# Modulation vectors on VectorE, attention scores on two row halves, and another order in the first mixer of a three-block forward pass

## The chip, the core and the metric

One NeuronCore of a Trainium2 chip runs the whole program: TensorE (PE; PEld is its weight load), VectorE (DVE), ScalarE (ACT), GpSimd (POOL) and SyncE (SP), which issues most DMAs. The metric is the device time of one execution in microseconds, as the median of several runs. TensorE's clock has two levels, 1.2 and 2.4 GHz; the profile gives the granted clock of a stretch as a fraction of the higher one. Everything is float32. Each product is made of three fp32r matmuls on a high and a low part of each operand (hi·hi, hi·lo, lo·hi), added up in PSUM.

## What is computed

A first block of three sub-blocks (feed-forward, mixer, feed-forward) acts on 512 rows of 1024 features; then come two layers, each with a mixer and a feed-forward. 256 context rows go beside the first of them. Each sub-block's input is normalized and changed by modulation vectors, which are products of one conditioning vector with large matrices. The part that the change touches:

```
# first mixer: 8 heads of 64, a band of 9 chunks of 64 keys, and a gated recurrence
q, k, v, xr, yr, g_att, g_rec = split(h @ w_in)
att = chunked_attention(q, k, v, rel_bias) @ w_att_o      # softmax(q k^T / 8 + bias) v
rec = (rg_lru(conv(xr), ...) * gelu(yr)) @ w_rec_o
merged = sigmoid(g_att) * att + sigmoid(g_rec) * rec

# layer mixers: 512 own keys and 256 context keys, head dimension 64
s = einsum('bqhgd,bkhd->bhgqk', gq, gk) * ATTN_SCALE      # 8 query heads, 2 key heads
p = softmax(s); o_g = einsum('bhgqk,bkhd->bqhgd', p, gv)
s = einsum('bqhjd,bkhjd->bhjqk', dq, dk) * ATTN_SCALE     # 4 heads of two score maps
a = softmax(s)[:, :, 0] - lam * softmax(s)[:, :, 1]; o_d = einsum('bhqk,bkhe->bqhe', a, dv)

# 27 modulation vectors of 1024, each silu(c) @ w[:, c0:c0+1024] + b
mod = (silu(c) @ w_ada + b_ada), (silu(c) @ w_mod + b_mod)
```

## The kernel before

The stages follow each other: a start (0 to 38 us of the profiled span), the first feed-forward (to 411), the first mixer (to 899), the second feed-forward with the context's mixer woven in (to 1585), the mixer of layer 0 (to 2310), its feed-forward (to 2913), the mixer of layer 1 (to 3638) and its feed-forward.

**Weights.** A step of the program (`Step`) names the weight blocks (`Unit`) that it needs. SP loads each block of 128x1024 into one of five `raw` buffers (L243 waits for a free one), in the order of the steps. `split` makes the high part on ScalarE (L282) and the low part on VectorE by a subtraction (L283). Products go through L309 to L311 and L321 to L323, and `esplit` splits a result (L326 on ScalarE, L328 or L330 on VectorE).

**Modulation vectors.** `mod` makes a vector out of eight pieces, each a plain `raw` block of 128x1024. `pieces` scales it by one column of the conditioning vector and adds it up: on GpSimd a scaling of the first (L383), and for each later one a scaling (L387) and an addition (L388); its other branch, on VectorE, is one fused multiply-add. `start` makes the first two vectors on VectorE by the same means (L405, L407). `turn` and `fin` then sum over the partitions and bring the row into shape. The vectors' steps are woven into the stages' bodies by `weave`, by each step's cost.

**Order.** Steps are merged by cost (`merge`, `weave`); within the program the order on PE, ACT and DVE is set by a scheduler at compile time, on SP and POOL it is as written. Each engine runs its instructions in order.

**First mixer** (`mixer1`). `front` runs the first products. Of `s_yr`, the eight products of the recurrent gate (Gelu at L787), four were its items; the other four, the values (`s_v`) and the queries and keys of the first pair of heads followed. Then 16 attention jobs (a head, and two query tiles) run through `skew`, whose stages are scores (L852) and the softmax's exponential (L862), scaling (L866 to L868), transposes (L1027), products with the values (L1051, L1052), and a fold (L1057 to L1063). `TUNE["soft"]["m"]` sets the order of these stages. The steps of the jobs were cut in four; three parts were merged with the queries and keys of the next pair (six products), the last with four steps of the recurrent part `s_rec` (convolution at L902 to L908, split at L910).

**Layer mixers** (`attend`). A job of "gqa" was one head and two query tiles; `scores` (L1313) wrote a bank `big` with products on one 64-row half, then the second bank. The keys `R["gk"]` held key head 0 on rows 0 to 63 and key head 1 on rows 64 to 127, and the query heads were laid out to match. In "diff" a job is a head and a query tile with both score maps, one on each half, and their banks were written one after the other. There are two `big` banks and four `mm` banks in PSUM.

Of the kernel before, what the change touches and what calls it, by code (L numbers as in the profile page):

```python
# [10 lines left out]
BF16 = mybir.dt.bfloat16  # L11
# [4 lines left out]
D = 1024  # L16
# [25 lines left out]
for _name, _w in (("qn", 64), ("kn", 64), ("dl", 256)):  # L42
# [24 lines left out]
    "soft": {"m": "scptf", "gc": "sptcf", "g0": "sptcf", "g1": "spctf", "dc": "scptn", "d0": "stcnp", "d1": "snptc"},  # L67
# [92 lines left out]
class K:  # L160
# [30 lines left out]
    def pair(self, n=512, kind=None):  # L191

        if n == 256:
            return self.half(F32R, kind).rearrange("p (a n) -> p a n", a=2)
        return self.s((2, n), F32R)

# [141 lines left out]
    def mod(self, key, w, c0, bias, ccol, gain=None, mult=None):  # L338
# [27 lines left out]
        steps = self.pieces(key, w, c0, ccol, begin, self.POOL)  # L366
# [407 lines left out]
    def mixer1(self, a, hk, yk, last):  # L774
# [7 lines left out]
        items = []  # L782
        for c, u in enumerate(self.units_a(w_in, 2560, D)):
# [4 lines left out]
            items.append((u, fn))  # L788
        items, s_yr = items[:4], [self.one(T, u, act, d) for u, d in items[4:]]
# [20 lines left out]
        s_qk = {}  # L810
        s_at = {}
        src = w_in.rearrange("(k p) c -> p k c", p=128)
        for i in range(4):
            us = [self.unit(src[:, :, j + i * 128:j + (i + 1) * 128]) for j in (0, 512)]
            s_qk[i] = []
            for j, u in enumerate(us):
                def fn(w, i=i, j=j):
                    ps = self.mm()
                    self.mma(ps, w, 0, act)
                    p = qk[i, j] = self.pair()  # L820
                    self.esplit(ps, p[:, 0, :], p[:, 1, :], 0.125 if j == 0 else 1.0)
                s_qk[i].append(Step(fn, [u]))
# [191 lines left out]
        steps += merge(cut[3], s_rec[:nr]) + drain  # L1014
# [50 lines left out]

    def skew(self, jobs, order, st_s, st_c, st_t, st_p, st_f=None, st_n1=None, st_n2=None):
# [5 lines left out]
        stages = [x for c in order for x in kinds[c]]  # L1072
        n, last = len(jobs), max(d for d, _, _ in stages)
        out = [[]]
        for i in range(n + last):
            for k, (d, f, pe) in enumerate(stages):
# [4 lines left out]
                if k == 0 and i < n:  # L1081
                    out.append([])
        steps, drain = out[:n], out[n]
        return steps, drain
# [52 lines left out]
    def rotate(self, out, x, nh, c, sn):  # L1137
# [4 lines left out]
        DVE.tensor_tensor(out, x, c.unsqueeze(1).to_broadcast([128, nh, 64]), ALU.mult)  # L1142
# [6 lines left out]
        DVE.tensor_tensor(out, out, t.rearrange("p (h d) -> p h d", h=nh), ALU.add)  # L1149
# [16 lines left out]
    def to_feat(self, src, T, scale=1.0, kind=None):  # L1166
# [4 lines left out]
        p = self.pair(T, kind)  # L1171
# [24 lines left out]
    def kv_gqa(self, w, T, act, rope, R, save=None):  # L1196
# [3 lines left out]
        def done(box):  # L1200
            gv = R["gv"] = self.pair(T).rearrange("p a n -> p (a n)").rearrange("p (t v x d) -> p t v x d", v=2, x=2, d=64)
            tk = self.e(T).rearrange("p (t d) -> p t d", d=128)
# [3 lines left out]
            for t, x in enumerate(self.head_norm([o[:, 0:128] for o in box["o"]], 2)):  # L1206
                o = tk[:, t, :].rearrange("p (h d) -> p h d", h=2)
                if rope:
                    self.rotate(o, x, 2, E["tab"][:, 1, 0, t, :], E["tab"][:, 1, 1, t, :])
# [746 lines left out]
```

## Time and profile before

| | us |
|---|---|
| median of three runs | 4000.06 |
| the three runs, from and to | 3992.86 to 4002.28 |
| the profiled execution, its own time | 4003.47 |
| its span in the trace | 4001.7 |

One execution was profiled. The views used below are the page with the busy time of each engine and the costliest groups of instructions, windows of busy time by stage (with the mean granted clock), groups by line with mean durations, single lines with minimum, median and maximum, waits, and the timeline of a stretch. In a group, `out<-in` are the program's tile names, `x` is a count, and the last column is idle time of the engine ahead of the group with what ended it.

### The profile page before, as it was taken

What the parts mean: (1) busy time and instruction counts of PE and PEld (TensorE: products, weight loads), DVE (VectorE), ACT (ScalarE), POOL (GpSimd) and SP (SyncE); (2) the same over time, 40 slices, a digit from 0 to 9 for tenths busy, and PEclk for the clock granted to TensorE, in tenths of its full rate; (3) what the DMA queues carried; (4) which work ended last, traced back from release to release, by engine and by line L of the source; (5) the groups of instructions that cost most, each with busy time, mean ns of one, the idle gap of its engine ahead of it and who ended that gap; (6) DMA issues with size and microseconds to landing.
All of it is one profiled execution on the core that took longest, in us unless ns stands there. A gap on an engine that the chain in (4) does not pass through costs nothing. (4 is left out here: it accounts for less than half of the span.)

```text
span 4001.7 us, 50668 instructions
## 1 busy us (share of the span) xinstructions
PE 3773.1 (94%) x19612; PEld 3196.3 (80%) x19612; DVE 2514.3 (63%) x3347; ACT 1533.9 (38%) x2437; POOL 1394.0 (35%) x1133
## 2 busy tenths in 40 slices
PE   7999987999899999899999989999998999899999
PEld 5888866778788887778887878888887887688887
DVE  5343478846766665957667466767587776655344
ACT  4222345533354443235433334333332543334322
POOL 1341364315844332451323144543146132312100
PEclk9999988999999999999999989999999999899999
DMA  6554533446455655221333356666532123333432
GB/s 226 155 160 128 152 113 116 145 127 194 149 160 173 187 168 176 80 82 41 106 95 95 121 166 198 195 200 195 170 104 82 56 85 96 106 121 114 127 103 94
DMA packets 534050, 536.26 MB, mean 134 GB/s; under 512 B 19696, under 2 KB 435696, under 8 KB 533808
## 3 DMA queue, kind: packets, MB, share of 16 engines
q1 hardware_dynamic: 517088, 487.48, 40.1%
q0 software_dynamic: 16720, 45.53, 3.5%
q8 instruction: 154, 2.52, 0.3%
q14 instruction: 88, 0.72, 0.1%
HBM read 507.66 MB, written 25.28 MB: 133 GB/s over the span
## 5 line engine op out<-in xcount | busy, mean ns | idle before, releaser
L283 DVE TENSOR_TENSOR wlo<-raw,whi 128x1024 fp32r<-128x1024 f32 (+3 forms) x674 | 921.9, 1370 | 803.1 <-ACT whi L282 783.6
L282 ACT ACTIVATE whi<-raw 128x1024 fp32r<-128x1024 f32 (+3 forms) x674 | 694.1, 1032 | 1551.6 <-PE mm L310 649.5
L309 PE MATMUL mm<-hT,whi 128*128 128x512 f32 (+1 forms) x2384 | 910.8, 385 | 44.4 <-ACT hT L326 11.0
L310 PE MATMUL mm<-hT,whi 128*128 128x512 f32 (+1 forms) x2384 | 907.1, 382 | 17.9 <-DVE hT L328 17.9
L311 PE MATMUL mm<-hT,wlo 128*128 128x512 f32 (+1 forms) x2384 | 902.9, 380 | 0.0
L309 PEld LDWEIGHTS mm<-hT,whi 128*128 128x128 f32 x2384 | 460.4, 195 | 132.4 <-ACT hT L326 14.0
L310 PEld LDWEIGHTS mm<-hT,whi 128*128 128x128 f32 x2384 | 463.2, 195 | 99.3 <-DVE hT L328 20.5
L311 PEld LDWEIGHTS mm<-hT,wlo 128*128 128x128 f32 x2384 | 462.6, 194 | 83.4 <-issue 0.4
L388 POOL TENSOR_TENSOR s<-s,raw 128x1024 f32<-128x1024 f32 x189 | 495.6, 2622 | 15.8
L387 POOL TENSOR_SCALAR raw<-raw,csil 128x1024 f32<-128x1024 f32 x189 | 281.4, 1489 | 380.9 <-DMA raw<-in_w_mod 191.2
L322 PE MATMUL mm<-wlo,s 128*128 128x512 f32 (+1 forms) x1004 | 371.4, 371 | 4.6 <-DVE wlo L283 4.6
L321 PE MATMUL mm<-whi,s 128*128 128x512 f32 (+1 forms) x1004 | 369.1, 371 | 0.0
L323 PE MATMUL mm<-whi,s 128*128 128x512 f32 (+1 forms) x1004 | 368.9, 370 | 0.0
L309 PE MATMUL mm<-s,whi 128*128 128x256 f32 (+1 forms) x1032 | 338.1, 329 | 10.9 <-ACT s L910 5.1
L310 PE MATMUL mm<-s,whi 128*128 128x256 f32 (+1 forms) x1032 | 333.1, 323 | 3.0 <-DVE s L328 3.0
L311 PE MATMUL mm<-s,wlo 128*128 128x256 f32 (+1 forms) x1032 | 332.0, 322 | 0.0
L309 PEld LDWEIGHTS mm<-s,whi 128*128 128x128 f32 x1032 | 199.2, 193 | 31.7 <-ACT s L910 5.5
L326 ACT ACTIVATE s<-mm 128x512 fp32r<-128x512 f32 (+2 forms) x302 | 156.7, 548 | 172.6 <-PE mm L1027 67.8
L322 PEld LDWEIGHTS mm<-wlo,s 128*128 128x128 f32 x1004 | 189.8, 189 | 37.1 <-DVE wlo L283 5.5
L321 PEld LDWEIGHTS mm<-whi,s 128*128 128x128 f32 x1004 | 189.8, 189 | 33.2 <-ACT eh L708 0.5
L323 PEld LDWEIGHTS mm<-whi,s 128*128 128x128 f32 x1004 | 189.8, 189 | 32.1 <-DVE s L690 0.4
L310 PEld LDWEIGHTS mm<-s,whi 128*128 128x128 f32 x1032 | 199.7, 194 | 19.2 <-DVE s L328 3.4
(334 smaller groups left out, 6179.6 us busy)
## 6 DMA issues: line engine op xcount, KB each, us to landing
raw<-in_w_in SPq DMA_DIRECT2D x231, 512.0 KB, 4.0
raw<-in_w_ff SPq DMA_DIRECT2D x188, 512.0 KB, 4.3
raw<-in_w_mod SPq DMA_DIRECT2D x160, 512.0 KB, 4.0
raw<-in_ffn_w_gu SPq DMA_DIRECT2D x88, 512.0 KB, 4.2
raw<-in_w_ada SPq DMA_DIRECT2D x72, 512.0 KB, 3.9
raw<-in_ffn_w_down SPq DMA_DIRECT2D x42, 512.0 KB, 3.8
raw<-in_w_out SPq DMA_DIRECT2D x32, 512.0 KB, 3.7
d_x<-s POOLq DMA_DIRECT2D x28, 512.0 KB, 4.8
```

Of the source, the lines that this page charges most:

```text
L282: self.ACT.activation(hi, v, ACTF.Copy)
L283: self.DVE.tensor_tensor(lo, v, hi.bitcast(F32), ALU.subtract)
L309: self.PE.matmul(out, hi[:, k, j:j + c], ah, start=start and k == 0, stop=False)
L310: self.PE.matmul(out, hi[:, k, j:j + c], al, start=False, stop=False)
L311: self.PE.matmul(out, lo[:, k, j:j + c], ah, start=False, stop=stop and k == nk - 1)
L321: self.PE.matmul(o, ah, hi[:, k, :], start=start and k == 0 and t % per == 0, stop=False)
L322: self.PE.matmul(o, ah, lo[:, k, :], start=False, stop=False)
L323: self.PE.matmul(o, al, hi[:, k, :], start=False, stop=stop and k == nk - 1 and t % per == per - 1)
L326: self.ACT.activation(hi, ps, ACTF.Copy, scale=scale)
L387: eng.tensor_scalar(v, v, c, 0.0, ALU.mult, ALU.add)
L388: eng.tensor_tensor(a, a, v, ALU.add)
```

## The change

1. `mod` has its pieces made on VectorE: 27 scalings (L389 in the new numbering) and 189 fused multiply-adds (L391) in place of GpSimd's instructions.
2. In the first mixer `front` takes the queries and keys of the first two pairs; the eight products of the recurrent gate and the other queries and keys are a list `side`, merged with the four first steps of `s_rec` through all 16 attention jobs. A job has three places for such work in place of one (the bars in `"s|ct|pf"`).
3. `scores` asks for both banks at once and alternates the matmuls between the row halves. A "gqa" job is now a pair of heads and one query tile (16 jobs, as before); the keys stand on both halves (`R["gk", v]`, with `twice` in `rotate`), for the context too, with a tile `cg` of their own. `fold_two` takes the place of `fold2` there (six operations for four). The weights of that branch are loaded as one block in place of two halves.
4. The tile `junk` becomes U8, which makes room for `cg`.

```
-        steps = self.pieces(key, w, c0, ccol, begin, self.POOL)
+        steps = self.pieces(key, w, c0, ccol, begin, self.DVE)
...
-    "soft": {"m": "scptf", ...
+    "soft": {"m": "s|ct|pf", ...
...
-        items, s_yr = items[:4], [self.one(T, u, act, d) for u, d in items[4:]]
+            s_yr.append(self.one(T, u, act, fn))
...
+                if i < 2:
+                    items.append((u, fn))
+                else:
+                    s_qk[i].append(self.one(T, u, act, fn))
...
-        steps = s_yr + s_v + s_qk[0]
-
-        n = len(at) // 4
-        cut = [at[i * n:(i + 1) * n] if i < 3 else at[3 * n:] for i in range(4)]
-        for i in range(3):
-            steps += merge(cut[i], s_qk[i + 1])
+        steps = list(s_v)
+
+        side = s_yr[:1] + s_qk[2] + s_yr[1:3] + s_qk[3] + s_yr[3:]
...
-        steps += merge(cut[3], s_rec[:nr]) + drain
+        steps += merge(at, side + s_rec[:nr]) + drain
...
-        def scores(ps, q, r0, h, t):
+        def scores(q, h, t):
+            pss = [self.big((1024,)) for _ in range(2)]
             for kp, o, n in keys(h):
                 for i, (x, y) in enumerate(((0, 0), (0, 1), (1, 0))):
-                    PE.matmul(ps[:, o:o + n], q[r0:r0 + 64, x, t * 128:(t + 1) * 128], kp[r0:r0 + 64, y, 0:n],
-                              start=i == 0, stop=i == 2)
+                    for c, ps in enumerate(pss):
+                        r = slice(64 * c, 64 * c + 64)
+                        PE.matmul(ps[:, o:o + n], q[r, x, t * 128:(t + 1) * 128], kp[r, y, 0:n], start=i == 0, stop=i == 2)
+            return pss
...
-            jobs = [(j + 4 * v, g, {}) for j in range(4) for v in range(2) for g in range(ng)]
+            jobs = [(c, t, {}) for c in range(4) for t in range(T // 128)]
...
-                r0, c = 64 * (h // 4), h % 4
-                if g == 0 and h < 4:
+                if t == 0:
                     oT[c] = self.pair(T, "o")
-                B["f"] = self.fold2(bo, oT[c], r0, g * 256, self.e(256 if T == S else 512))
+                B["f"] = self.fold_two(bo, oT[c], t * 128, self.e(256 if T == S else 512))
...
-            R["gk"] = self.to_feat(lambda t: tk[:, t, :], T)
+            for v in range(2):
+                p = self.cg().rearrange("p (a n) -> p a n", a=2) if T != S and v else None
+                R["gk", v] = self.to_feat(lambda t: tk[:, t, v * 128:(v + 1) * 128], T, p=p)
```

Where the instructions stand is shown at three places; a row has the line, the operation, out<-in and the shape.

GpSimd in the first mixer's attention before: the softmax scalings (L867), loads of bias tiles (L836, L837) and a vector's pieces (L387, L388).

```order
L867 TENSOR_SCALAR e_4082<-e_4082,st_4079 128x256
L387 TENSOR_SCALAR raw_3857<-raw_3857,csil 128x1024
L388 TENSOR_TENSOR s_4052<-s_4052,raw_3857 128x1024
L365 DMA dG_4141<-row_3509 32x32
L867 TENSOR_SCALAR e_4172<-e_4172,st_4169 128x512
L836 MEMSET e_4202 64x192
L837 DMA e_4202<-in_relb 64x448
L836 MEMSET e_4202 64x128
L837 DMA e_4202<-in_relb 64x512
L387 TENSOR_SCALAR raw_3918<-raw_3918,csil 128x1024
L388 TENSOR_TENSOR s_4052<-s_4052,raw_3918 128x1024
```

GpSimd at the same place now:

```order
L874 TENSOR_SCALAR e_3809<-e_3809,st_3806 128x256
L874 TENSOR_SCALAR e_3892<-e_3892,st_3889 128x512
L843 MEMSET e_3958 64x192
L844 DMA e_3958<-in_relb 64x448
L843 MEMSET e_3958 64x128
L844 DMA e_3958<-in_relb 64x512
L874 TENSOR_SCALAR e_3974<-e_3974,st_3971 128x256
L352 DMA row_4046<-in_b_ada 32x32
L874 TENSOR_SCALAR e_4070<-e_4070,st_4067 128x512
L371 DMA dG_4126<-row_3554 32x32
L843 MEMSET e_4168 64x192
```

The pieces are gone from it. VectorE at the same place now (L391 pieces, L875 softmax scaling, L864 the read of a score bank, L289 a weight's low part):

```order
L391 SCALAR_TENSOR_TENSOR s_4045<-raw_3931,csil,s_4045 128x1024
L1067 TENSOR_TENSOR s_4030<-eh_4031,s_4030 64x256
L391 SCALAR_TENSOR_TENSOR s_4045<-raw_4043,csil,s_4045 128x1024
L873 RECIPROCAL st_4067<-st_4067 128x2
L289 TENSOR_TENSOR wlo_4251<-raw_4120,whi_4250 128x256
L366 TENSOR_TENSOR row_3554<-mm_4122,row_3554 32x32
L391 SCALAR_TENSOR_TENSOR s_4045<-raw_4055,csil,s_4045 128x1024
L875 TENSOR_SCALAR e_4068<-e_4068,st_4067 128x512
L334 TENSOR_TENSOR s_4110<-mm_4105,s_4110 128x512
L369 SCALAR_TENSOR_TENSOR row_3554<-row_3554 32x32
L391 SCALAR_TENSOR_TENSOR s_4045<-raw_4114,csil,s_4045 128x1024
L864 ISA e_4182,st_4180<-big_4173,e_3958 128x256
```

The pieces stand between the attention's own instructions, each behind the load of its `raw` block.

TensorE at a score step of "gqa" in layer 0 before: L1027 are transposes of probabilities, L1313 the scores of two `big` banks.

```order
L1027 MATMUL mm_15621<-ident,e_15460 128x128
L1027 MATMUL mm_15621<-ident,e_15462 128x128
L1313 MATMUL big_15642<-s_13935,s_14089 128x512 x3
L1313 MATMUL big_15642<-s_14404,s_14089 128x256 x3
L1313 MATMUL big_15649<-s_13935,s_14089 128x512 x3
L1313 MATMUL big_15649<-s_14404,s_14089 128x256 x3
L1027 MATMUL mm_15629<-ident,e_15460 128x128
L1027 MATMUL mm_15629<-ident,e_15462 128x128
```

The same step now (L1031 transposes, L1345 scores):

```order
L1345 MATMUL big_14722<-s_13862,s_13927 128x512
L1345 MATMUL big_14723<-s_13862,s_13927 128x512
L1345 MATMUL big_14722<-s_13862,s_13927 128x512
L1345 MATMUL big_14723<-s_13862,s_13927 128x512
L1345 MATMUL big_14722<-s_13862,s_13927 128x512
L1345 MATMUL big_14723<-s_13862,s_13927 128x512
L1345 MATMUL big_14722<-s_14339,s_13927 128x256
L1031 MATMUL mm_14709<-ident,e_14572 128x128
L1031 MATMUL mm_14709<-ident,e_14574 128x128
L1031 MATMUL mm_14709<-ident,e_14572 128x128
L1031 MATMUL mm_14709<-ident,e_14574 128x128
L1345 MATMUL big_14723<-s_14339,s_13927 128x256
```

The products of two banks alternate where they were three and three; the first 256-column product stands ahead of four transposes, the other five behind them.

ScalarE at the start of the first mixer's attention before: L282 a weight's high part, L326 copies, L862 the exponential.

```order
L326 ACTIVATE s_3338<-mm_3212 128x8x64
L282 ACTIVATE whi_3411<-raw_3343 128x1024
L326 ACTIVATE s_3376<-mm_3351 128x512
L282 ACTIVATE whi_3515<-raw_3415 128x1024
L326 ACTIVATE s_3404<-mm_3379 128x512
L326 ACTIVATE s_3489<-mm_3464 128x512
L862 ACT_TABLE_LOAD
L862 ACTIVATE e_3436,st_3435<-e_3436,st_3434 128x256
L862 ACTIVATE e_3438,st_3435<-e_3438,st_3434 128x256
L862 ACTIVATE e_3455,st_3454<-e_3455,st_3453 128x512
L862 ACTIVATE e_3457,st_3454<-e_3457,st_3453 128x512
L326 ACTIVATE s_3500<-mm_3495 128x512
```

And now (L793 is the gate's Gelu, L869 the exponential):

```order
L288 ACTIVATE whi_3418<-raw_3308 128x1024
L793 ACT_TABLE_LOAD
L793 ACTIVATE s_3242<-mm_3217 128x512
L332 ACTIVATE s_3277<-mm_3272 128x512
L869 ACT_TABLE_LOAD
L869 ACTIVATE e_3294,st_3293<-e_3294,st_3292 128x256
L869 ACTIVATE e_3296,st_3293<-e_3296,st_3292 128x256
L288 ACTIVATE whi_3547<-raw_3416 128x1024
L332 ACTIVATE s_3335<-mm_3310 128x512
```

The Gelu, which was complete ahead of the attention, now stands between exponentials, with a table load at each turn.

## Rows read from the trace of the kernel before

**Rows 1.** The page, busy time of each engine, its share, and instructions.

```profile
PE 3773.1 (94%) x19612; PEld 3196.3 (80%) x19612; DVE 2514.3 (63%) x3347; ACT 1533.9 (38%) x2437; POOL 1394.0 (35%) x1133
```

**Rows 2.** Windows of three stages; columns as in the first line.

```profile
core 0: us, PE busy (x) PEld busy (x) DVE busy (x) ACT busy (x) POOL busy (x), PEclk, DMA share, GB/s
...
411.00:899.00 488.00, 442.03 (x2010) 360.50 (x2010) 323.21 (x423) 217.16 (x351) 191.03 (x175) 0.93 0.43 130
...
1585.00:2310.00 725.00, 675.63 (x3653) 571.38 (x3651) 497.52 (x753) 271.41 (x459) 229.91 (x188) 0.95 0.31 91
...
2913.00:3638.00 725.00, 678.08 (x3654) 571.96 (x3654) 499.63 (x749) 271.40 (x461) 237.94 (x193) 0.95 0.30 91
```

**Rows 3.** Groups by line and shape, GpSimd: busy us, mean ns, idle before.

```profile
L388 POOL TENSOR_TENSOR s<-s,raw 128x1024 f32<-128x1024 f32 x189 | 495.6, 2622 | 15.8
...
L383 POOL TENSOR_SCALAR s<-raw,csil 128x1024 f32<-128x1024 f32 x27 | 35.8, 1325 | 137.3 <-DMA raw<-in_w_ada 51.2 <-DMA raw<-in_w_mod 37.2 <-PE mm L1052 26.6
```

**Rows 4.** VectorE by group (mean) and by single line (minimum/median/maximum ns).

```profile
L283 DVE TENSOR_TENSOR wlo<-raw,whi 128x1024 fp32r<-128x1024 f32 (+3 forms) x674 | 921.9, 1370 | 803.1 <-ACT whi L282 783.6
...
L283 DVE TENSOR_TENSOR wlo<-raw,whi x674: 398/1225/3440, 37.2 to 3972.5; 128x1024 fp32r<-128x1024 f32 x161, 128x768 fp32r<-128x768 f32 x6, 128x256 fp32r<-128x256 f32 x1, 128x512 fp32r<-128x512 f32 x1
...
L690 DVE TENSOR_TENSOR s<-e,s 128x512 fp32r<-128x512 f32 x108 | 91.4, 847 | 25.3 <-ACT s L689 25.1
...
L690 DVE TENSOR_TENSOR s<-e,s x108: 643/686/2903, 56.3 to 3942.2; 128x512 fp32r<-128x512 f32 x108
...
L328 DVE TENSOR_TENSOR s<-mm,s 128x512 fp32r<-128x512 f32 x222 | 147.1, 682 | 43.8 <-ACT s L326 42.5
```

**Rows 5.** The line L908, and the timeline at 732 us: start, duration, [idle before].

```profile
L908 DVE SCALAR_TENSOR_TENSOR s<-s,cols,s x24: 719/752/2778, 594.3 to 737.0; 128x512 f32<-128x512 f32 x24
...
732.49 2.45 POOL L388 TENSOR_TENSOR s<-s,raw 128x1024 f32<-128x1024 f32 x1
...
732.72 7.04 DVE L908 SCALAR_TENSOR_TENSOR s<-s,cols,s 128x512 f32<-128x512 f32 x3
...
740.50 0.77 PE L309 MATMUL mm<-s,whi 128*128 128x512 f32 x1 [5.08 <-ACT s L910]
```

**Rows 6.** Timeline of TensorE: the first and the last gap of the 51.

```profile
529.13 0.36 PE L1051 MATMUL mm<-s,s 128*128 128x256 f32 x1 [1.05 <-DVE s L330]
...
3637.97 0.58 PE L310 MATMUL mm<-hT,whi 128*128 128x256 f32 x1 [3.88 <-DVE hT L328]
```

**Rows 7.** Groups by line: the multiply-add in the kernel's start.

```profile
L407 DVE SCALAR_TENSOR_TENSOR s<-raw,csil,s 128x1024 f32<-128x1024 f32 x14 | 18.0, 1289 | 3.0 <-DMA raw<-in_w_ada 2.6
```

**Rows 8.** The tile raw: who waited for it (us, times), and its DMAs.

```profile
  POOL raw L387: 281.1, 41
...
  POOL s L383: 101.5, 11
...
DMA to landing us min/median/max: 2.0/4.0/11.5
```

**Rows 9.** Timeline of TensorE: three runs of score products.

```profile
1147.86 0.97 PE L1313 MATMUL big<-s,s 64*128 64x256 f32 x6
...
1287.12 0.63 PE L1313 MATMUL big<-s,s 64*128 64x256 f32 x6
...
1843.73 2.37 PE L1313 MATMUL big<-s,s 64*128 64x512 f32 x12
```

**Rows 10.** Groups by line and shape: all score products of the layer mixers.

```profile
L1313 PE MATMUL big<-s,s 64*128 64x512 f32 x384 | 120.9, 439 | 10.3 <-ACT e L1322 10.3
...
L1313 PE MATMUL big<-s,s 64*128 64x256 f32 x480 | 82.8, 292 | 0.0
```

**Rows 11.** Windows in the first mixer's attention, columns as in rows 2.

```profile
497.00:550.00 53.00, 49.88 (x229) 37.90 (x229) 39.65 (x86) 26.58 (x60) 33.63 (x37) 0.90 0.35 104
550.00:640.00 90.00, 64.75 (x281) 51.02 (x280) 77.14 (x131) 46.76 (x96) 52.47 (x50) 0.79 0.37 109
```

**Rows 12.** ScalarE's table load at L787; TensorE's waits from 497 to 640 us.

```profile
L787 ACT ACT_TABLE_LOAD x1 | 1.3, 1283 | 0.0
...
PE mm L1051 <- ACT s L326: 11.9, 5, 8.9
```

More of the change, by code (lines that the diff above doesn't have):

```diff
@@ L1064, in fold2, with fold_two, fn @@
         return fn
+    def fold_two(self, ps, pair, c0, t):
+        t = t[:, 0:128]
+        for i in range(2):
+            self.ACT.activation(t[64 * i:64 * i + 64], ps[64 - 64 * i:128 - 64 * i, 128 * i:128 * i + 128], ACTF.Copy)
+        for i in range(2):
+            v = t[64 * i:64 * i + 64]
+            self.DVE.tensor_tensor(v, ps[64 * i:64 * i + 64, 128 * i:128 * i + 128], v, ALU.add)
+        def fn():
+            h, lo = (pair[:, x, c0:c0 + 128] for x in range(2))
+            self.ACT.activation(h, t, ACTF.Copy)
+            self.DVE.tensor_tensor(lo, t, h.bitcast(F32), ALU.subtract)
+        return fn
     def skew(self, jobs, order, st_s, st_c, st_t, st_p, st_f=None, st_n1=None, st_n2=None):
@@ L1071, in skew @@
                  "f": [(2, st_f, 0.1)], "n": [(3, st_n1, 1.5), (4, st_n2, 1.5)]}
-        stages = [x for c in order for x in kinds[c]]
+        order = order if "|" in order else order[0] + "|" + order[1:]
+        stages = [x for c in order if c != "|" for x in kinds[c]]
+        cuts = {sum(len(kinds[c]) for c in o if c != "|") - 1 for o in (order[:i] for i, c in enumerate(order) if c == "|")}
         n, last = len(jobs), max(d for d, _, _ in stages)
@@ L1080, in skew @@
                     out[-1].append(Step(fn, need=("big",) if k == 0 else ("mm",) if pe > 0.1 else (), pe=pe))
-                if k == 0 and i < n:
+                if k in cuts and i < n:
                     out.append([])
-        steps, drain = out[:n], out[n]
-        return steps, drain
+        return out[:-1], out[-1]
     def layer_setup(self, a, l, rope):
@@ L1148, in rotate @@
                               sv[:, :, i, :].unsqueeze(1).to_broadcast([128, nh, 2, 16]), ALU.mult)
-        DVE.tensor_tensor(out, out, t.rearrange("p (h d) -> p h d", h=nh), ALU.add)
+        th = t.rearrange("p (h d) -> p h d", h=nh)
+        if twice:
+            o, th = (v.unsqueeze(2).to_broadcast([128, nh, 2, 64]) for v in (o, th))
+        DVE.tensor_tensor(out, o, th, ALU.add)
     def head_norm(self, xs, nh):
@@ L1301, in keys @@
             if kind == "gqa":
-                own, ctx = R["gk"], C["gk"] if C else None
+                own, ctx = R["gk", h // 4], C["gk", h // 4] if C else None
             else:
@@ L1373, in st_s @@
         def st_s(h, g, j, B, b):
-            pss = []
-            for c in range(2):
-                ps = self.big((1024,))
-                scores(ps, R["dq", h], 64 * c, h, 2 * g + j)
-                pss.append(ps)
-            softmax(pss, b)
+            softmax(scores(R["dq", h], h, 2 * g + j), b)
         def st_c(h, g, j, B, b):
@@ L1679, in mixer2 @@
         w3 = lambda n: self.units_a(a[n][l], 0, D, 256)
-        gsrc = a["w_br_gqa_2"][l].rearrange("(v j d) c -> v d j c", v=2, j=4)
-        def gunit(c0):
-            return Unit(lambda raw: [(raw[v * 64:(v + 1) * 64], gsrc[v][:, :, c0:c0 + 256]) for v in range(2)], 4, 256)
-        ug = [gunit(c0) for c0 in range(0, D, 256)]
         keep = sv if ctx else None
```

89 lines of the change are left out of this document (42 added, 47 removed).

## The prediction, made before the changed kernel was run

> **What bounds the kernel now.** I read the busy shares first: TensorE is busy for 94% of the span, VectorE for 63%, ScalarE for 38%, GpSimd for 35% [rows 1]. So TensorE's own work is the floor, and time can be gained in three places only: matmuls that could share the array, stretches in which TensorE waits, and stretches in which its granted clock is at the lower of its two levels, 1.2 instead of 2.4 GHz. The windows by stage show where the last two are [rows 2]. In the first mixer TensorE is idle for 488 − 442 = 46 us, and the mean granted clock of 0.93 costs 0.07 × 488 = 34 us more. In the two layer mixers idle is 49 and 47 us, and the clock of 0.95 costs 36 us each. The three together have 142 us idle and 106 us lost to the clock, 0.75 us of clock for each us of idle. The feed-forward stages, which the list leaves out, are tighter.
>
> Next I asked what VectorE does ahead of those gaps. The commonest work, the subtraction that makes a weight's low part, has a median of 1225 ns, a mean of 1370 and a maximum of 3440. A subtraction of two SBUF tiles in the feed-forward stages has 686, 847 and 2903. An addition of the same size that reads PSUM has a mean of 682 [rows 4]. The timeline shows what the long ones stand beside: three convolution taps (median 752 ns, maximum 2778) take 7.04 us while GpSimd adds a modulation piece, and the next matmul starts after 5.08 us of idle that ends with that convolution [rows 5]. Those additions are 189 and take 495.6 us [rows 3]. The two groups above hold 674 × 0.145 + 108 × 0.161 = 98 + 17 = 115 us of stretch on VectorE. On TensorE I went through all gaps over 0.15 us and kept those that start within 4 us behind a stretched VectorE operation, counting no more of a gap than that stretch: 51 gaps, 80 us. The first and the last of them are in [rows 6].
>
> **Part 1, the modulation pieces go from GpSimd to VectorE.** This removes the 189 scalings and 189 additions, and 27 first pieces, from GpSimd [rows 3]. On VectorE it adds 189 fused multiply-adds and 27 scalings. The start of the kernel already runs the multiply-add there, at 1289 ns [rows 7], and a scaling does less: 216 × 1.289 = 278 us at most. VectorE would go from 2514 to 2792 us, less the stretch that goes (at least the 115), so to 2677 or less of a span near 3900, 69%; it stays off the bound on average. What goes is the stretch that these additions cause. GpSimd's other additions, the taps of the layers' convolutions, stay. I count half of the 80 us, 40: some of those gaps have another cause too, and a new piece of 1.29 us can itself stand ahead of an operation for which TensorE waits. Each us of idle costs up to 0.75 us of clock; I take 0.35, under half, because part of the low clock lies in work on 64 rows with no gap near it. 40 × 1.35 = **−54 us**. The ends: 0 if new pieces delay as much as they free, −80 × 1.75 = −140 if every gap goes.
>
> The order shows what queues behind a new wait. In the mixer's attention GpSimd had the pieces between the softmax scalings; now VectorE has four among twelve instructions, ahead of the scaling that the next transposes wait for and of the read of the next score bank. A piece waits for a raw weight block from a DMA; behind it in VectorE's order stand that scaling and that read, and TensorE behind them. What GpSimd waited for such blocks is 281.1 us in 41 waits and 101.5 us in 11 [rows 8]. In front of GpSimd's waits stood little work; on VectorE each piece has other work ahead, in the mixer mostly over 4.5 us of it between the release of the buffer and the piece by my own addition along the new order, beside a median of 4.0 us to landing [rows 8]. In the feed-forward stages the lead is often shorter, but there VectorE has more slack. So I cost the wait at 0, covered by that lead; its price without the cover is the fourth rival.
>
> **Part 2, scores on two row halves at once.** In the order of before a bank's products stand three and three on one half; now two banks on opposite halves alternate. The trace has the pair of cases: six 64x256 products on one half take 0.97 us, six that alternate take 0.63, so a pair saves 0.34 / 3 = 0.113 us. Six of 512 columns and six of 256 on one half take 2.37 us, so one of 512 takes (2.37 − 0.97) / 6 = 0.233 us, and that is the most that a pair of these can save [rows 9]. Of 192 pairs of 512 and 240 of 256 (half of [rows 10]'s counts) the new order has 106 and 140 next to each other; in the rest the second bank comes later, and the products stand block after block as before. 106 × 0.233 + 140 × 0.113 = 41 us, less some 3 us for the few that already alternate: **−37 us**. The ends: 0 if 512-column products don't overlap and the switches cost the rest, −69 if all 432 pairs did. The Trainium skill (TensorEngine Tiling (Array Packing), Theoretical Speedup) gives "up to 2×" for a dimension of at most 64; 0.97 to 0.63 is 1.5×, and by the full 2× the 246 pairs would give some 7 us more.
>
> **Part 3, the first mixer's order.** Between 497 and 640 us, where its attention jobs run, TensorE is idle for 143 − 114.6 = 28 us, and the clock costs 0.10 × 53 + 0.21 × 90 = 24: 52 us together [rows 11]. One wait there, for the copy that follows the transposes, is 8.9 us [rows 12]. Ten products or steps stood between the jobs before (six of queries and keys, four of the recurrent part); now sixteen do, with all eight of the recurrent gate. Part 1 has 18 of the 52 us already (half of the 26 us of its gaps that lie in this stage, × 1.35). Of the other 34 I take half: **−17 us**, ends 0 and −34. It is no more than half, since VectorE is busy for 77 of the 90 us there.
>
> **What is added.** The gate's Gelu now alternates with the softmax's Exp on ScalarE, and the order has 13 more table loads in all. At 1283 ns [rows 12] that is 17 us on an engine that is 38% busy. Key tiles are made for both halves (12 more transposes and two split copies for one), and a fold has six short operations for four. I take **+5 us** of these on the path (0 to +22, if all table loads and the transposes lie on it).
>
> **The sum:** −54 − 37 − 17 + 5 = −103 us. The profiled execution took 4003.5 us by its own time (span 4001.7); 4003.5 − 103 = 3900. The median of three runs is 3.4 us lower, so I forecast 3897.
>
> **Rivals.**
> First, the pieces cost VectorE what their stretch cost it: up to 278 us is added, the stretch that I can show is 115. Then −54 becomes 0, and the time 3951. For it: VectorE is at 77 of 90 us in the mixer's attention [rows 11]. Against it: the stretch falls on operations for which TensorE waits, pieces are wanted late and can slip. The Trainium skill (Perfetto Trace Analysis, Optimizing Scalar/DVE Operations) speaks against the move: the two engines share an SBUF read port, so moving operations between them "might not help"; by that the time would be this rival's. The trace agrees as to the port ([rows 4]: 847 ns from SBUF beside 682 from PSUM).
> Second, alternating halves gain nothing at 512 columns or in the changed surroundings: 3897 + 37 = 3934. For it: no such run of 512 is in the trace. Against it: the 0.63 us row.
> Third, all the gaps close: −140 in place of −54, so 3811. For it: GpSimd's small operations (a norm's root, the scaling of probabilities) also no longer queue behind 2.4 us additions.
> Fourth, slower: VectorE is held in order by the raw blocks. GpSimd's 382.6 us of such waits [rows 8] move to an engine that TensorE needs. If 40% of it reaches TensorE, 153 − 103 = +50 and the time is 4050. It decides from 103 / 382.6 = 27%. Against it: the lead above.
> Fifth, the three gains fall on stretches that other waits end anyway, and the time stays near 4000.
>
> **How the numbers follow.** Forecast 45%, first rival 18%, second 8%, third 15%, fourth 9%, fifth 5%. A measurement of this kernel can tell about 0.3%, 12 us, from no change. Slower then has 10% (the fourth, and a part of the fifth), same 5%, faster 85%. The range 3820 to 3972 leaves out the fourth and fifth rival and the far end of the third.
>
> **What the profile after would show.** Part 1: the mean of the low-part subtraction falls from 1370 to near 1230, fused multiply-adds stay near 1.3 us, GpSimd falls below 1394 − 496 = 898 us, the 5.08 us gap is gone. If instead VectorE shows long waits for raw blocks at the pieces, the fourth rival holds. Part 2: twelve products of a score pair in 1.2 to 1.5 us where they alternate, and the sum over all scores down by 37. Part 3: in the attention of the first mixer the granted clock rises from 0.79 towards 0.9 and TensorE's idle halves. The forecast is wrong if the idle of the three mixers stays at 142 us.

## The result

The changed kernel takes 3882.74 us (3877.93 to 3887.33) beside 3999.66 for the kernel before: a ratio of 0.971, 95% interval 0.969 to 0.973, 117 us less. The forecast was 3897, 103 less. The profiled execution of after took 3877.93 us with a span of 3876.1, 125.6 less than the span of before. Of all the runs reported below one is left out, an execution of e11 that took 4517 us at a granted clock of 0.76.

The page of after, busy time by engine (it answers to [rows 1]):

```profile
PE 3697.3 (95%) x19624; PEld 3143.1 (81%) x19624; DVE 2470.4 (64%) x3607; ACT 1549.4 (40%) x2494; POOL 597.5 (15%) x732
```

GpSimd is down to 15%. VectorE runs 260 instructions more; its pieces alone take 243 + 21 = 264 us, and yet it is busy for 44 us *less* than before. So some 308 us of its 2514 had been stretch: time by which an operation takes longer than its usual duration.

The windows of after for the first mixer, the second feed-forward, the mixer of layer 0, its feed-forward and the mixer of layer 1, cut where each stage's first product starts; three answer to [rows 2]:

```profile
411.50:854.30 442.80, 420.67 (x2009) 346.66 (x2009) 302.32 (x462) 232.15 (x363) 47.69 (x98) 0.98 0.47 143
854.30:1523.50 669.20, 651.58 (x3868) 573.74 (x3868) 445.36 (x678) 293.20 (x487) 138.65 (x169) 0.99 0.59 177
1523.50:2227.40 703.90, 657.72 (x3657) 556.32 (x3657) 492.22 (x796) 271.63 (x476) 146.80 (x143) 0.96 0.31 95
2227.40:2809.40 582.00, 573.00 (x3114) 497.20 (x3114) 375.14 (x469) 237.12 (x360) 61.70 (x92) 0.99 0.63 194
2809.40:3512.20 702.80, 659.66 (x3657) 559.13 (x3657) 499.32 (x790) 270.49 (x477) 151.89 (x147) 0.95 0.31 95
```

The second feed-forward, the mixer of layer 0 and its feed-forward in the kernel before, for comparison:

```profile
899.00:1584.50 685.50, 660.03 (x3866) 580.52 (x3866) 459.99 (x621) 293.15 (x478) 317.60 (x256) 0.98 0.57 172
1584.50:2310.30 725.80, 676.14 (x3654) 571.88 (x3654) 498.32 (x755) 271.94 (x460) 230.21 (x189) 0.95 0.31 91
2310.30:2913.00 602.70, 582.76 (x3112) 502.14 (x3112) 390.21 (x420) 235.82 (x359) 247.21 (x180) 0.98 0.61 187
```

Read the first number behind each window, the stage's length. The first mixer lost 45 us, the second feed-forward 16, layer 0's mixer 22, its feed-forward 21, layer 1's mixer 22; the other stages stand still. In the first mixer idle went from 46 to 22 us and the granted clock from 0.93 to 0.98. In the two layer mixers idle hardly moved (50 to 46, 47 to 43), nor did the clock: there TensorE's busy time fell, by 18 us each.

VectorE's groups and single lines of after (they answer to [rows 4, 5, 7]; L289 is a weight's low-part subtraction, L696 the subtraction of two SBUF tiles in the feed-forward stages, L391 the pieces, L912 the convolution tap):

```profile
L289 DVE TENSOR_TENSOR wlo<-raw,whi 128x1024 fp32r<-128x1024 f32 (+3 forms) x674 | 812.8, 1208 | 656.7 <-ACT whi L288 643.8
...
L289 DVE TENSOR_TENSOR wlo<-raw,whi x674: 413/1224/2307, 37.6 to 3846.6; 128x1024 fp32r<-128x1024 f32 x161, 128x768 fp32r<-128x768 f32 x6, 128x256 fp32r<-128x256 f32 x1, 128x512 fp32r<-128x512 f32 x1
...
L391 DVE SCALAR_TENSOR_TENSOR s<-raw,csil,s 128x1024 f32<-128x1024 f32 x189 | 243.1, 1286 | 178.4 <-DMA raw<-in_w_mod 120.8 <-DMA raw<-in_w_ada 56.9
...
L696 DVE TENSOR_TENSOR s<-e,s x108: 646/686/693, 56.6 to 3816.3; 128x512 fp32r<-128x512 f32 x108
...
L912 DVE SCALAR_TENSOR_TENSOR s<-s,cols,s x24: 714/750/754, 574.7 to 695.7; 128x512 f32<-128x512 f32 x24
```

The medians are those of before; the maxima are gone (2903 to 693, 2778 to 754 ns). The one line that keeps a long maximum, 2307, has its long ones (five over 2 us) in the layer mixers, beside GpSimd's convolution taps (a scaling at L1557, an addition at L1558), which the change left there, as this piece of the timeline of after shows (start, duration):

```profile
2913.12 1.57 POOL L1558 TENSOR_TENSOR s<-s 128x512 f32<-128x512 f32 x1
2913.49 2.28 DVE L289 TENSOR_TENSOR wlo<-raw,whi 128x1024 fp32r<-128x1024 f32 x1
```

TensorE's score products of after, by shape, and four runs of them (they answer to [rows 9, 10]):

```profile
L1345 PE MATMUL big<-s,s 64*128 64x512 f32 x384 | 93.6, 464 | 17.4 <-ACT e L1354 17.2
...
L1345 PE MATMUL big<-s,s 64*128 64x256 f32 x456 | 65.7, 304 | 0.0
...
1717.23 0.97 PE L1345 MATMUL big<-s,s 64*128 64x512 f32 x6
...
1737.69 1.90 PE L1345 MATMUL big<-s,s 64*128 64x512 f32 x12
1742.44 1.31 PE L1345 MATMUL big<-s,s 64*128 64x512 f32 x6 [1.40 <-ACT e L1354]
...
1958.61 1.31 PE L1345 MATMUL big<-s,s 64*128 64x512 f32 x12
```

Six products of 512 columns that alternate take 0.97 us; by [rows 9] six of them added 2.37 − 0.97 = 1.40 to a run on one half. Twelve that alternate, six of each width (1958.61), take 1.31 us, and so do the six of a single bank (1742.44, which came after a wait for the exponential that reads a bank). So the products on the second half cost no time where the two alternate, for 512 columns as well. Of the 42 unbroken runs of twelve 23 take 1.3 us. In the run at 1737.69 the start times show each bank's six products in a block, the second block 0.58 us behind the first: 1.90 us.

### The profile page after: what moved, and what is told of

The parts are those of the page before. It is cut to its first block, busy times and chain, and to the rows that moved or that the text cites. A ratio compares the mean times of both kernels' runs of the same rounds, so it can differ in the third digit from the quotient of the medians.

```text
span 3876.1 us, 50566 instructions
## 1 busy us (share of the span) xinstructions
PE 3697.3 (95%) x19624; PEld 3143.1 (81%) x19624; DVE 2470.4 (64%) x3607; ACT 1549.4 (40%) x2494; POOL 597.5 (15%) x732
## 5 line engine op out<-in xcount | busy, mean ns | idle before, releaser
L289 DVE TENSOR_TENSOR wlo<-raw,whi 128x1024 fp32r<-128x1024 f32 (+3 forms) x674 | 812.8, 1208 | 656.7 <-ACT whi L288 643.8
L391 DVE SCALAR_TENSOR_TENSOR s<-raw,csil,s 128x1024 f32<-128x1024 f32 x189 | 243.1, 1286 | 178.4 <-DMA raw<-in_w_mod 120.8
L317 PEld LDWEIGHTS mm<-s,wlo 128*128 128x128 f32 x1032 | 198.3, 192 | 14.0
```

The lines of the kernel that those rows point to most:

```text
L289: self.DVE.tensor_tensor(lo, v, hi.bitcast(F32), ALU.subtract)
L317: self.PE.matmul(out, lo[:, k, j:j + c], ah, start=False, stop=stop and k == nk - 1)
L391: eng.scalar_tensor_tensor(a, v, c, a, ALU.mult, ALU.add)
```

## The experiments

Each is compared with the kernel before, run on the same chip beside it; a difference from the changed kernel is taken between the two ratios, times 4000 us, and is uncertain by some 10 us.

**Each part alone, and the largest undone.** e1_pieces_only is the kernel before with

```
-        steps = self.pieces(key, w, c0, ccol, begin, self.POOL)
+        steps = self.pieces(key, w, c0, ccol, begin, self.DVE)
```

> The kernel before with one change: the modulation pieces on VectorE. Theory: the trace of after is 126 us shorter than that of before, of which 37 lie in the score products and 45 in the first mixer; the second feed-forward (-13 without scores), the feed-forward of layer 0 (-21) and the layer mixers (-9 without scores) can come from the pieces alone, and some 20 of the first mixer's 45. So about -63 us, 3937 (3920 to 3955). Rival, that the new multiply-adds cost VectorE what the stretch cost it: within 15 us of 4000. Rival, that the pieces are all of the first mixer's gain too: -88, 3912. The mean of the low-part subtraction should fall from 1370 to near 1210 ns in any case.

Measured: 3925.98 beside 4001.46, ratio 0.981 (0.9795 to 0.9825), 75 us less, between the theory's 63 and the second rival's 88. The first rival is out. Its page, its windows (first mixer, second feed-forward, and layer 0's mixer, its feed-forward and layer 1's mixer) and its low-part subtraction:

```profile
PE 3742.7 (95%) x19612; PEld 3181.1 (81%) x19612; DVE 2478.4 (63%) x3563; ACT 1533.9 (39%) x2437; POOL 596.7 (15%) x728
...
410.10:873.90 463.80, 433.74 (x2010) 357.96 (x2010) 303.92 (x462) 216.41 (x351) 49.65 (x97) 0.95 0.45 137
873.90:1546.30 672.40, 652.04 (x3865) 575.27 (x3865) 445.49 (x669) 293.02 (x478) 139.57 (x168) 0.99 0.59 176
1546.30:2265.00 718.70, 675.77 (x3654) 570.92 (x3654) 497.30 (x779) 272.32 (x460) 146.03 (x145) 0.96 0.31 92
2265.00:2848.10 583.10, 573.19 (x3111) 497.41 (x3111) 374.28 (x468) 236.00 (x358) 60.66 (x90) 0.99 0.63 193
2848.10:3561.50 713.40, 673.85 (x3654) 570.17 (x3654) 501.82 (x773) 271.34 (x461) 149.99 (x148) 0.95 0.31 93
...
L283 DVE TENSOR_TENSOR wlo<-raw,whi 128x1024 fp32r<-128x1024 f32 (+3 forms) x674 | 814.1, 1210 | 681.5 <-ACT whi L282 665.7 <-PE mm L1027 7.1 <-PE mm L310 3.4
```

The pieces alone take 24 us from the first mixer, 13 from the second feed-forward and 20 from layer 0's feed-forward, all of what these last two lost in after but 3 and 1 us; from the layer mixers they take 7 and 12. Over the span TensorE's idle falls from 228.6 to 182.3 us, and its busy time by 30 us for the same 19612 products, at a mean granted clock of 0.973 in place of 0.964.

e2_halves_only is the kernel before with `scores`, the jobs, keys and folds of the change, and nothing else.

> The kernel before with one change: scores alternate between the row halves (with the jobs, keys and folds that belong to it). Theory: the score products take 37 us less from start to start, and all of it shows, since TensorE is busy for 94%: 3963 to 3970. Rival, that the freed time turns into waits for the softmax or for split weights while the pieces are still on GpSimd: less than half of it, 3982 or more.

Measured: 3977.05, ratio 0.9939 (0.9922 to 0.9955), 24 us less, between the two. Summed from the start of a score product to the start of TensorE's next matmul, each counted as 0.6 us at most, these products take 169 us in the trace of before, 134 here and 132 in after: the 35 to 37 us are gained in full.

```profile
PE 3740.1 (94%) x19624; PEld 3167.5 (80%) x19624; DVE 2514.7 (63%) x3391; ACT 1534.5 (39%) x2481; POOL 1403.4 (35%) x1137
```

TensorE's busy time falls by 33 us, and its idle grows from 228.6 to 235.0, so that the span is 27 shorter.

e3_order_only is the kernel before with `"s|ct|pf"`, `items`, `side` and the merge of the change.

> The kernel before with one change: the first mixer's order. Theory: by itself about -17 us, 3983, in the first mixer alone. Rival 1, that the order does most of the first mixer's 45: -35 to -45, 3955 to 3965. Rival 2, that the order pays only where the pieces are off GpSimd, since the softmax scalings there still queue behind 2.4 us additions: within 8 us of 4000.

Measured: 3990.61, ratio 0.9973 (0.9963 to 0.9984), 11 us less. The interval, 6 to 15 us, holds the second rival's 8 and leaves out the theory's 17. In the trace the first mixer is 11 us shorter.

e4_pieces_back is the changed kernel with `self.POOL` again.

> The changed kernel with one part undone: the pieces on GpSimd again. If the parts add up, it loses what the pieces alone gained: 3883 + 63 = 3946 by the theory, 3883 by the first rival of e1, 3971 by its second. More than that would show that the denser first mixer suffers more from the pieces on GpSimd than the old one.

Measured: 3965.74, ratio 0.9907 (0.9892 to 0.9922), 79 us more than the changed kernel, nearest to the second rival's 3971. The parts alone give 75 + 24 + 11 = 110 us, together 117: close to a sum, with the surplus in the first mixer. There the row of e4 reads

```profile
409.90:887.20 477.30, 428.49 (x2009) 351.89 (x2009) 328.51 (x422) 235.11 (x366) 195.49 (x174) 0.94 0.44 133
```

477.3 against 487.7 of before: the order takes 10 us with the pieces on GpSimd, but 463.8 − 442.8 = 21 with them on VectorE.

**What in the pieces costs.** e5_dummy_additions is the changed kernel with

```
                 elif eng is self.DVE:
                     eng.scalar_tensor_tensor(a, v, c, a, ALU.mult, ALU.add)
+                    z = self.ident.unsqueeze(1).to_broadcast([128, 4, 128])
+                    for _ in range(2):
+                        self.POOL.tensor_tensor(self.dum..., z, z, ALU.add)
```

> The changed kernel, and beside each of the 189 fused multiply-adds GpSimd makes two additions of 128x512 on constants, into a tile that nothing reads. They hold no raw block and nobody waits for their result; only VectorE's access to SBUF and GpSimd's own queue are burdened as before. Theory, that VectorE's stretch beside GpSimd's two-input additions was the cost of the pieces: most of the 83 us that undoing the move cost come back, 3930 to 3965, and the mean of the low-part subtraction rises from 1208 to 1330 ns or more. Rival, that the cost was the raw block which GpSimd held too long (SyncE waited for these additions 325 us in 91 waits): at most +20, 3903.

Measured: 3961.91 beside 3994.68, ratio 0.9919 (0.9904 to 0.9934), 84 us more than the changed kernel: as much as undoing the move. No raw block is held by these additions, so the rival falls. VectorE's operations on two SBUF tiles stretch (L289, L391, L699), those of L334, which read PSUM, do not. The mean of the subtraction rose, though to 1286 and not to 1330; the pieces are stretched too.

```profile
L394 POOL TENSOR_TENSOR dum<-ident 128x512 bf16<-128x512 f32 x378 | 500.5, 1324 | 23.8
...
L289 DVE TENSOR_TENSOR wlo<-raw,whi 128x1024 fp32r<-128x1024 f32 (+3 forms) x674 | 864.7, 1286 | 598.8 <-ACT whi L288 580.9 <-DMA raw<-in_w_ff 8.4 <-PE mm L316 3.5
L391 DVE SCALAR_TENSOR_TENSOR s<-raw,csil,s 128x1024 f32<-128x1024 f32 x189 | 260.3, 1377 | 166.8 <-DMA raw<-in_w_mod 106.3 <-DMA raw<-in_w_ada 59.8
...
L334 DVE TENSOR_TENSOR s<-mm,s 128x512 fp32r<-128x512 f32 x224 | 148.2, 684 | 23.4 <-ACT s L332 21.4
L699 DVE TENSOR_TENSOR s<-e,s 128x512 fp32r<-128x512 f32 x108 | 81.7, 757 | 21.9 <-ACT s L698 21.7
```

e9_dummy_scalings has `for _ in range(3)` and `self.POOL.tensor_scalar(self.dum..., z, 2.0, 0.0, ALU.mult, ALU.add)` in that place.

> As e5, but in place of two additions of 128x512 GpSimd makes three scalings of 128x512 (one tile read in place of two), for about the same 500 us of GpSimd's time. In the kernel before, VectorE's operations beside 495.6 us of additions held 206 us over their usual duration, and beside 281.4 us of scalings 47 us: 0.42 and 0.17 us for each us. Theory, that the cost is VectorE's access to SBUF beside GpSimd and goes with this stretch: 0.17 / 0.42 of e5's 83 us, about +33, 3912 (3900 to 3925). Rival, that GpSimd's queue (its small operations for norms and softmax behind the long ones) was the cost in e5: the same +83, 3962.

Measured: 3920.96 beside 4000.69, ratio 0.9802 (0.9788 to 0.9815), 37 us more than the changed kernel. GpSimd is as busy with them as with the additions, so its queue is as long; what differs is the operation, a scaling with one tile input or an addition with two.

```profile
L394 POOL TENSOR_SCALAR dum<-ident 128x512 bf16<-128x512 f32 x567 | 493.0, 870 | 41.4
...
L289 DVE TENSOR_TENSOR wlo<-raw,whi 128x1024 fp32r<-128x1024 f32 (+3 forms) x674 | 840.8, 1250 | 627.7 <-ACT whi L288 615.7 <-PE mm L1034 3.4 <-PE mm L316 3.3
```

The Trainium skill (GPSIMD Engine Reference, Key points) has GpSimd share its SBUF interfaces with VectorE, with contention for VectorE's instructions in a two-port mode or with two SBUF inputs. The trace of e5 agrees as to the two inputs (757 ns at L699 beside 684 at L334), and e9 adds that GpSimd's one-input scalings cost under half of its additions (37 us beside 84).

I summed, over all VectorE instructions of a trace, the time beyond the fast fifth of their kind (the 20th percentile, and 60 ns more):

| kernel | stretch, us | time against the changed kernel, us |
|---|---|---|
| after | 57 | 0 |
| e4, pieces back | 334 | +79 |
| e5, additions | 208 | +84 |
| e9, scalings | 124 | +37 |
| e10, taps moved | 10 | −23 |

Three kernels that differ from the changed one chiefly in what GpSimd does beside VectorE cost 84 / 151 = 0.56, 37 / 67 = 0.55 and 23 / 47 = 0.49 us for each us of stretch. With GpSimd's queue as long in e9 as in e5, a cost that goes with the stretch alone fits both; within the uncertainty some 15 us could be the queue's. The move itself comes out cheaper: undoing it brings 277 us of stretch (before has 329) and costs 79, or 99 with the 20 us that VectorE's own pieces cost (e8 below), 0.36 us for each.

**What the pieces cost VectorE.** e8_short_pieces is the changed kernel with `a[:, 0:32], v[:, 0:32], c, a[:, 0:32]` in the fused multiply-add.

> The changed kernel with each fused multiply-add cut to 32 of its 1024 columns; most of the modulation vectors is left out. It still waits for the raw block and frees it. This takes some 189 x 1.2 = 227 us from VectorE. Theory, that VectorE has room for them: no more than 15 us less, 3868 to 3883. Rival, my first one from before (the pieces cost VectorE what they free): 40 us less or more, below 3843.

Measured: 3860.9 beside 3994.68, ratio 0.9661 (0.9645 to 0.9677), 20 us less than the changed kernel, a little over the theory's 15 and half of the rival's 40 (10 to 30 with the uncertainty). Its pieces:

```profile
L391 DVE SCALAR_TENSOR_TENSOR s<-raw,csil,s 128x32 f32<-128x32 f32 x189 | 49.1, 260 | 203.1 <-DMA raw<-in_w_mod 141.0 <-DMA raw<-in_w_ada 61.2
```

243 − 49 = 194 us of VectorE's work are worth 20 us, about one in ten.

e12_no_raw_pieces is the changed kernel with

```
+                v = raw[:, 0, :]... if i == 7 else self.ident.unsqueeze(1).to_broadcast([128, 8, 128])
...
-        return [Step(piece(i), [self.unit(...)], need=(), pe=1.0) for i in range(8)]
+        return [Step(piece(i), [self.unit(...)] if i == 7 else [], need=(), pe=1.0) for i in range(8)]
```

> The changed kernel with seven of each vector's eight pieces computed from a constant tile in place of a raw block: the modulation vectors are not the right ones, 189 loads of 512 KB are left out, and VectorE's multiply-adds stay at full length and wait for no load. What is left out is more than the waits (less DMA traffic, raw buffers free for weights), so this bounds from above what the pieces' waits for raw blocks on VectorE cost, 178 us by the trace of after. Theory, that these waits lie in VectorE's own slack: within 20 us of after, 3863 to 3883. Rival, my fourth one (a third or more of the waits reaches TensorE): 50 us less or more, below 3833.

Measured: 3871.74 beside 4001.23, ratio 0.9675 (0.9659 to 0.9691), 14 us less. The tile raw of after has the waits in question, and that of this run has those that are left, at each vector's eighth piece:

```profile
  DVE s L391: 177.7, 81
```

```profile
  DVE s L392: 32.8, 14
```

The waits did move to VectorE, but of the 145 us that went no more than 14, 10%, cost time (17% with the uncertainty), and less by what the missing loads save.

**The other two parts.** e6_block_order is the changed kernel with

```
+            for c, ps in enumerate(pss):
+                r = slice(64 * c, 64 * c + 64)
                 for kp, o, n in keys(h):
                     for i, (x, y) in enumerate(((0, 0), (0, 1), (1, 0))):
-                    for c, ps in enumerate(pss):
-                        r = slice(64 * c, 64 * c + 64)
```

> The changed kernel with one thing undone: the same jobs, keys and banks, but the six matmuls of one bank stand before the six of the other. Theory, that the overlap of the two row halves is the gain of this part: the score products take 35 us more, and 25 to 30 us of it show, 3908 to 3915. Rival, that the gain is in the jobs themselves (a pair of heads and one query tile, natural layout): within 8 us of 3883.

Measured: 3898.93 beside 3994.68, ratio 0.9758 (0.9744 to 0.9773), 19 us more than the changed kernel; its score products take 155 us by the sum above, 23 more, where I expected 35, and 25 to 30 of it in the time. The overlap is the gain, and not the new jobs: of the 864 score products 66 start within 0.06 us of the one ahead in the trace of before, 286 in that of after, and 142 here. So the blocks of two banks still overlap at places, with 76 pairs more than in before and 14 us less, beside 220 pairs and 37 us in after.

```profile
L1345 PE MATMUL big<-s,s 64*128 64x512 f32 x384 | 113.7, 451 | 12.1 <-ACT e L1354 12.1
...
L1345 PE MATMUL big<-s,s 64*128 64x256 f32 x456 | 78.3, 297 | 0.0
```

e7_order_back is the changed kernel with the first mixer's code of before.

> The changed kernel with the first mixer's order undone. Theory, that the order pays twice as much once GpSimd is free of the pieces (the first mixer takes 21 us less than with the pieces alone, against 11 us in e3): 3904 with all of it in the first mixer. Rival, that the parts add up: +11, 3894.

Measured: 3909.18 beside 3994.68, ratio 0.9782 (0.9768 to 0.9797), 29 us more than the changed kernel. The rival that the parts add up is out; the first mixer takes 462.1 us in its trace, 19 more than in after. The other 10 lie outside it, where the theory had none, and are within the uncertainty.

e11_gelu_in_twos is the changed kernel with

```
-        side = s_yr[:1] + s_qk[2] + s_yr[1:3] + s_qk[3] + s_yr[3:]
+        side = [s_yr[:2]] + s_qk[2] + [s_yr[2:4]] + s_qk[3] + [s_yr[4:6], s_yr[6:]]
```

> The changed kernel with the recurrent gate's eight products placed two by two between the attention's steps, which takes 6 table loads of 1.283 us (46 in place of 52). Theory, that the table loads lie on an engine with room: within 5 us of 3883. Rival, that they delay the exponentials on which the attention waits: 6 to 10 us less. Against both, the work between the jobs is lumpier: some us more.

Measured: 3884.72 beside 4000.69, ratio 0.9717 (0.9704 to 0.973): no difference from the changed kernel within the 10 us, which is more than the 8 us that six table loads last. So this leaves the price of a table load open, and a saving by the loads and a loss by the lumpier order could cancel too.

**A version that beats both.** e10_taps_on_vector is the changed kernel with

```
-                        (DVE if c < 2 else self.POOL).tensor_scalar(acc, vp[:, 0:T], wc, ...)
+                        DVE.tensor_scalar(acc, vp[:, 0:T], wc, ...)
-                    elif c < 2:
-                        DVE.scalar_tensor_tensor(acc, vp[:, j:j + T], wc, acc, ALU.mult, ALU.add)
                     else:
-                        v = R["a", 1][:, 1, :T]
-                        self.POOL.tensor_scalar(v, vp[:, j:j + T], wc, 0.0, ALU.mult, ALU.add)
-                        self.POOL.tensor_tensor(acc, acc, v, ALU.add)
+                        DVE.scalar_tensor_tensor(acc, vp[:, j:j + T], wc, acc, ALU.mult, ALU.add)
```

> The changed kernel with the third of the layers' convolution taps on VectorE too, as fused multiply-adds, in place of a scaling and an addition on GpSimd (90 taps, 118 us of additions before). VectorE gets 60 x 0.74 + 30 x 0.47 = 59 us and loses the stretch beside them, 47 us by the trace of after. Theory, that the stretch costs where TensorE waits and VectorE has room: some 5 to 15 us less than after, 3868 to 3878. Rival, that VectorE in the layer mixers (497 of 704 us busy, and 120 taps of its own there) has no room: 0 to +20, 3883 to 3903.

Measured: 3860.73 beside 4000.69, ratio 0.9653 (0.964 to 0.9666), 23 us less than the changed kernel and more than the 5 to 15 that I expected. The page of it, and its taps, with those of after (120) as the last line:

```profile
PE 3686.0 (96%) x19624; PEld 3137.0 (81%) x19624; DVE 2467.1 (64%) x3700; ACT 1549.7 (40%) x2494; POOL 363.3 (9%) x549
...
L1554 DVE SCALAR_TENSOR_TENSOR s<-s,dwh,s 128x512 f32<-128x512 f32 x180 | 125.7, 740 | 0.0
```

```profile
L1554 DVE SCALAR_TENSOR_TENSOR s<-s,dwh,s 128x512 f32<-128x512 f32 x120 | 109.2, 949 | 0.0
```

VectorE does half as many taps again and is busy for 3 us less: a tap fell from 949 to 740 ns.

## Why the prediction was right, and where its terms were off

**The time.** 3883 lies 14 us from the forecast, in the main case, in part by luck: part 1 was too small by some 21 us and part 2 too large by some 13.

**Part 1, −54: too small.** The pieces are worth 75 us alone and 79 undone. The mechanism was right, and the whole of the idle nearly so; the term that was mis-sized is the clock's share, 0.35 us for each us of idle. What went from TensorE in e1, in us, beside what the prediction took (half of its gaps, sorted by stage in the trace of before, and 0.35 of that):

| stage | idle, taken | idle, e1 | busy time, taken | busy time, e1 |
|---|---|---|---|---|
| first mixer | 13 | 16 | 5 | 8 |
| second feed-forward | 6 | 5 | 2 | 8 |
| layer 0's mixer | 10 | 7 | 3 | 0 |
| layer 0's feed-forward | 2 | 10 | 1 | 10 |
| layer 1's mixer | 9 | 7 | 3 | 4 |
| sum | 40 | 45 | 14 | 30 |

TensorE's busy time fell by 30 us where 14 were taken: 0.67 for each us of idle, near the 0.75 that the prediction had as the most. In the two feed-forward stages the granted clock rose from 0.98 to 0.99, though the prediction called them tighter and read the clock in the mixers alone. The one stage where the count of gaps itself failed is layer 0's feed-forward: 4 us of gaps stood within 4 us behind a stretched operation, and 10 us of idle went. By what way the rest of that idle hung on the stretch was not tried.

The stretch itself I put at "at least 115" by two groups; with 264 us added and 44 fewer busy it was near 308 (272 by the sum above, which leaves out 60 ns of each operation). That was the first rival's whole ground. e8 gives its price: the added work costs 20 us, the stretch that went cost some 95 (75 + 20). By the Trainium skill (Perfetto Trace Analysis, Optimizing Scalar/DVE Operations) moving work between these two engines might not help, since they share a port; here it helped by 75 us: one fused operation took the place of two, and GpSimd's had held VectorE up for somewhat longer (308 us) than the work takes there (264), on operations that cost more (95 us beside 20).

**Part 2, −37: right in its products, too large in time.** The sum of the 246 pairs was met (169 to 132 us), but alone 24 us showed (18 to 31), and 19 of the 23 that e6 takes away, which the uncertainty leaves open to be all. The step that failed is that all of the 37 us shows in the time: in the layer mixers of after idle is still 46 and 43 us, and in e2's trace idle grew by 6 us while the products shrank. The second rival is out by the rows of 0.97 and 1.31 us. The prediction's 1.5 to 1 came from runs of six with their first and last product whole; by the 1.31 us, for twelve as for six, the saving of 0.113 and 0.233 us for a pair was already all that the overlap can give, and the 7 us more were not to be had.

**Part 3, −17: about right, for a reason that I had only in part.** It is −11 with the pieces on GpSimd and −21 (by the windows of e1 and after) to −29 (by e7) without them. My sum took it as a term of its own, what part 1 leaves over; it depends on part 1, without which it is worth about half. In the attention the picture is as forecast: the window of before from 480 to 640 us and of after from 480 to 625,

```profile
480.00:640.00 160.00, 131.62 (x583) 102.99 (x583) 122.67 (x224) 77.74 (x161) 86.10 (x86) 0.85 0.36 106
```

```profile
480.00:625.00 145.00, 132.67 (x641) 106.54 (x640) 116.10 (x225) 92.51 (x165) 21.82 (x46) 0.95 0.47 138
```

have idle of 28 and 12 us and granted clocks of 0.85 and 0.95.

**What was added, +5:** no run settles it. e11 found nothing to gain from six table loads, but could not have told 8 us, and the transposes and folds were not measured apart.

**The fourth rival** had its mechanism right and its price wrong: 177.7 us of waits came to stand on VectorE, under half of the 382.6, and of the 145 that e12 takes away at most 14 us cost time, where 103 was needed. That the lead ahead of the pieces is what covered them fits this, but no run changed the lead.

**The signs that I named** came as said for the subtraction (1208), the pieces (1286), GpSimd (597.5), twelve score products (1.31 us), their sum (37 us less) and the first mixer. The idle of the three mixers fell from 142 to 111, three quarters of it in the first. One sign failed: the gap of 5.08 us behind the convolution is not gone. Its taps take at most 754 ns now, and TensorE still waits there:

```profile
697.20 0.73 PE L315 MATMUL mm<-s,whi 128*128 128x512 f32 x2 [3.74 <-ACT s L914]
```

In e1, which has the order of before, the wait is 3.1 us. So the stretch of those taps was the smaller part of that gap.

## What to carry to other kernels

Look for VectorE operations whose mean is well over their median, and see what GpSimd does beside the long ones; if it adds two SBUF tiles there, moving that to VectorE as one fused operation can shorten VectorE's own busy time. Price such a stretch by its whole sum too, and not only by the gaps that stand right behind it: here each us of it cost 0.36 us of the kernel by the move and about half a us by the three others, though not in every stage (the first feed-forward lost 15 us of it by the same sum and stayed at 373 us). Where idle goes, look at TensorE's busy time as well: with the granted clock it gave back another 0.67 us for each. A reordering can be worth more after such a cause is gone than before, so the parts of a change should be tried in each other's company and not only alone.

## What was unexpected

GpSimd's work that nobody waits for cost 84 us in 500 us of two-input additions, but 37 in 493 us of one-input scalings. Taking 118 us of additions with their scalings from GpSimd gave VectorE 90 more multiply-adds, and it was busy for 3 us less. And in the layer mixers TensorE's granted clock stayed at 0.96 and 0.95 in after (0.95 and 0.95 before), though over half of VectorE's stretch there was gone (99 to 43 us by the sum above). In e10, where 4 us of it are left, it is 0.96 in both; what holds it down was not tried.
